# Six projected tiles traced with the first RWKV iterations, another SBUF layout, and GLA and SSD in three passes

## The chip, the cores and the metric

The kernel runs on one core of a Trainium2 chip. The metric is the device time of one execution in microseconds; before the change it is 2274.1 us (median of 3 runs, 2272.3 to 2274.61).

## What is computed

Two layers over 256 context and 1024 image tokens of width 1024. Each layer normalizes, projects once, feeds four token mixers of width 256, and projects back:

```python
hn = rmsnorm(h, p['norm_pre']) * (1.0 + scale) + shift
proj = hn @ p['w_in']
f_rw, f_s5, f_ssd, f_gla = split_last(proj, [...])
y_rw, st_rw = rwkv7_mixer(f_rw, p, grid, ini[0], need_out)
y_s5, st_s5 = s5_mixer(f_s5, p, ini[1], need_out)
y_ssd, st_ssd = ssd_mixer(f_ssd, p, ini[2], need_out)
y_gla, st_gla = gla_mixer(f_gla, p, ini[3], need_out)
y = jnp.concatenate([y_rw, y_s5, y_ssd, y_gla], axis=-1) @ p['w_out']
return h + gate * rmsnorm(y, p['norm_post']), states
```

Every mixer runs forwards and backwards; the context's final states start the image's scan, and layer 1 needs no output for the context. GLA and SSD are chunked linear recurrences (chunks of 64 and 128 tokens): each chunk contributes a state, `S = dec * S + ctb`, and a chunk's output is a term within the chunk plus the query times the state before the chunk. RWKV7 has a recurrence with a rank-one correction, which the kernel solves per window of 128 tokens with a triangular inverse.

## The kernel before

A layer has three stages, `project`, `rw` and `out_proj`, with SBUF pools of their own (`pools`), opened on the left or the right side of SBUF. A pool that opens over a closed one waits, tile by tile, for the old tile's last reader (`reuse_waits="tile"`). All code is traced in program order; the framework's scheduler then fixes one static order of instructions on each engine, which the chip runs in order.

`project` keeps the normalized input split in two fp32r halves (`hi`, `lo`: the tile pool `hn`) and multiplies it with weight tiles that are also split (`i_wh`, `i_wl`): three products, summed in the PSUM bank `pj`. The stage does S5's constants, GLA, SSD and RWKV's shifted projections (order `MO = 'pgsr'`), and at its end the last six tiles: `u0`, `u1` (S5's input), `s5g0`, `s5g1` (its gate), `rwg0`, `rwg1` (RWKV's gate). Results go to DRAM (`f_...`, `rm`). Then `hn` is closed.

GLA before goes through 20 steps `s`. Each transposes keys when needed (`g_kp`), multiplies the query chunk with the state `g_S` (`pc<-g_S,g_e`, one 64x256 program for each direction), adds the result to `g_Y` on VectorE, multiplies keys and values into a contribution (`pc<-l_gv,g_kp`), and forms the next state from PSUM in two products on VectorE (`g_S`, `g_Sd`). SSD does the same in 10 steps, with a state `s_S` that ACT copies out of `s_Sc`.

`rw` runs ten windows in each direction as a software pipeline of 14 iterations: `elem` (decays, `ps<-r_in`, `r_BK`), `pair` (`pb<-r_AD,r_BK`, the matrices `r_A`), the inversion (`r_N`, `r_X`, `r_tp` on VectorE, `pi<-r_DN,r_Am` on TensorE), the chain through the state (`px<-r_UV,r_A`, `px<-r_S,r_AR`, `pu`), and `rw_final`, which norms and gates (`r_yt`, `qfy`) and stores to `yd`. S5's scan runs beside it in pieces.

`out_proj` loads 16 half tiles of `w_out` through a stage of two buffers (`o_w`), splits each (ACT casts `o_w0h`..., POOL or VectorE subtracts to `o_w0l`...), loads `yd` (`o_y`), splits it, and accumulates 192 matmuls for each block of 256 tokens.

Of the kernel before, what the change touches and what calls it, by code (L numbers as in the profile page):

```python
# [15 lines left out]
OP = mybir.AluOpType  # L16
# [219 lines left out]
RL = ('sm rp rl hp tp qp|re rx', 're hp tp qp rx|rp sm rl')  # L236
CL = ('oy oo ob|oa', 'oa oy oo|ob')
# [11 lines left out]

LE = "vvvv"  # L250

AL = "hp sm rp tp qp"


class K:
# [133 lines left out]
    def gla(self, src, outs):  # L389
# [20 lines left out]
        gall, gs = self.S("gall", [128, 2, 20, 4]), self.S("g_gs", [128, 2, 20])  # L410
        k, q = src["gk"], src["gq"]
        for d in range(2):
# [19 lines left out]
            if d == 0:  # L432
                self.tt(g[:, 0:19], l3[:, 0:19], em[:, 1:20], OP.mult)
                nc.vector.tensor_copy(g[:, 19:20], l3[:, 19:20])
            else:
                self.tt(g[:, 0:3], l3[:, 3:0:-1], em[:, 2::-1], OP.mult)
                self.tt(g[:, 3:4], l3[:, 0:1], em[:, 19:20], OP.mult)
                self.tt(g[:, 4:19], l3[:, 19:4:-1], em[:, 18:3:-1], OP.mult)
                nc.vector.tensor_copy(g[:, 19:20], l3[:, 4:5])
            self.tt(gall[:, d], g.unsqueeze(2).to_broadcast([128, 20, 4]),  # L440
                    c("bm4").unsqueeze(1).to_broadcast([128, 20, 4]), OP.mult)
# [7 lines left out]
        Y = [self.T("g_Y", [128, 5, 256]) for _ in range(2)]  # L449
        St = Sp = None  # L450
        for s in range(20):
            ch = [s, 3 - s if s < 4 else 23 - s]
            jb = [x // 2 for x in ch]
            if s % 2 == 0:

                kp = next(kring)
                ps = self.P()
                for d in range(2):
                    nc.tensor.transpose(ps[:, d * 128:(d + 1) * 128], ke[d][:, jb[d] * 128:(jb[d] + 1) * 128], c("ident"))
                p3 = ps[:, :256].rearrange("p (a b) -> p a b", a=2)  # L460
                nc.scalar.copy(kp[0:64, :, 0, :], p3[0:64])
                nc.vector.tensor_copy(kp[64:128, :, 1, :], p3[64:128])
                first = s == 0 if s < 4 else s < 12
                if first and (outs or s >= 4):
                    for j in (jb if jb[0] != jb[1] else jb[:1]):
                        self.gla_pair(j, qe, ke, next(pring), V, Y)
            if s > 0 and (outs or s >= 4):

                ps = self.P("pc")[:, :256]
                for d in range(2):  # L470
                    r = 64 * (ch[d] % 2)
                    self.mm(ps[r:r + 64], qe[d][:, ch[d] * 64:(ch[d] + 1) * 64], St[:, d, :])
                for d in range(2):
                    j, r = jb[d], 64 * (ch[d] % 2)
                    y = Y[j // 5][r:r + 64, j % 5, :]
                    self.tt(y, ps[r:r + 64], y, OP.add)
            if s == 19:
                break
            ps = self.P("pc")[:, :128]
            for d in range(2):  # L480
                j, r = jb[d], ch[d] % 2
                for h in range(4):
                    self.mm(ps[32 * h:32 * h + 32, d * 64:(d + 1) * 64], kp[:, d, r, 32 * h:32 * h + 32], V[j // 5][:, j % 5, h * 64:(h + 1) * 64])

# [28 lines left out]
    def gla_pair(self, j, qe, ke, pa, V, Y):  # L513

        nc, c = self.nc, self.c
        pm = []
        halves = [slice(0, 64), slice(64, 128)]
        for d in range(2):
            qb = self.Q("g_qb", [128, 4, 128])
            self.tt(qb, qe[d][:, j * 128:(j + 1) * 128].unsqueeze(1).to_broadcast([128, 4, 128]),  # L520
                    c("bm4").unsqueeze(2).to_broadcast([128, 4, 128]), OP.mult, "p")
            ps = self.P()[:, :256]
            for h in halves:
                self.mm(ps[h], ke[d][:, j * 128 + h.start:j * 128 + h.stop], qb[:, :, h])
# [7 lines left out]
        ps = self.P()  # L532
        for h in range(4):
            self.mm(ps[:, h * 64:(h + 1) * 64], pa[:, h, :], V[j // 5][:, j % 5, h * 64:(h + 1) * 64])
        nc.scalar.copy(Y[j // 5][:, j % 5, :], ps[:, :256])  # L535


    def ssd(self, src, outs):
# [60 lines left out]
        Y = [self.T("s_Y", [128, 5, 256]) for _ in range(2)]  # L599
        cring = self.ring("s_cp", [128, 2, 128], 2)  # L600
        sring = self.ring("s_S", [128, 2, 256], 2)
# [7 lines left out]
        St = Sp = None  # L609
        for s in range(10):  # L610
            tl = [s, 1 - s if s < 2 else 11 - s]
            if (s == 0 or 2 <= s < 6) and (outs or s >= 2):
                for j in tl:
                    self.ssd_pair(j, B, C, next(cring), xt, stri, lap, dt, Y)
            if s > 0 and (outs or s >= 2):
                ps = self.P("pc")
                for d in range(2):
                    self.mm(ps[:, d * 256:(d + 1) * 256], C[:, tl[d] * 128:(tl[d] + 1) * 128], St[:, d, :])
                yt = self.Q("s_yt", [128, 2, 256])
                for d in range(2):  # L620
                    j = tl[d]
                    y = Y[j // 5][:, j % 5]
                    self.tt(yt[:, d].rearrange("p (h v) -> p h v", h=4), ps[:, d * 256:(d + 1) * 256].rearrange("p (h v) -> p h v", h=4),
                            ex[:, 0, d, j].unsqueeze(2).to_broadcast([128, 4, 64]), OP.mult)
                    self.tt(y, y, yt[:, d], OP.add, "p")
            if s == 9:
                break
            ps = self.P("pc")
            xw = self.Q("s_xw", [128, 2, 4, 64])
            for d in range(2):  # L630
                j = tl[d]
# [6 lines left out]
            p3 = ps[:, :256].rearrange("p (d h v) -> p d h v", d=2, h=2)  # L638
            Sc = self.S("s_Sc", [128, 2, 2, 64], bufs=2)
            if Sp is None:  # L640
                nc.vector.tensor_copy(Sc, p3)
            else:
                self.tt(Sc, Sp, dc[:, :, s].unsqueeze(3).to_broadcast([128, 2, 2, 64]), OP.mult)
                self.tt(Sc, p3, Sc, OP.add)
            Sn = next(sring)
            for g in range(2):
                a = slice(64 * g, 64 * g + 64)
                nc.scalar.copy(Sn[a, :, 128 * g:128 * g + 128].rearrange("p d (h v) -> p d h v", h=2), Sc[a])
            St, Sp = Sn, Sc
# [373 lines left out]
    def rpool(self, name):  # L1023
        return getattr(self, self.where.get(name, "rp"))
# [25 lines left out]
    def rw_proj(self, n, hi, lo, outs):  # L1050
# [6 lines left out]
        for b, (b0, m) in enumerate(BLK):  # L1057
# [4 lines left out]
            o = self.R("i_o", [128, 512], 5)[:, :m]  # L1062
# [32 lines left out]
    def rw_mixed(self, n, kind, o, b0):  # L1095
# [24 lines left out]
    def rw(self, outs, side={}):  # L1120
# [3 lines left out]
        for p, ns in (("re", "in th a cs eP BK AD Ad N X Am tp Rm Bb"), ("rx", "AR A"), ("rl", "ks yt fin f0 yw")):  # L1124
            self.where.update({"r_" + n: p for n in ns.split()})
# [14 lines left out]
        for i in range(10 + 4):  # L1140
            with ExitStack() as es:
# [28 lines left out]
    def rw_elem(self, W):  # L1170
# [62 lines left out]
    def rw_pair(self, W):  # L1233
# [3 lines left out]
        A = self.R("r_A", [128, 2, 4, 2, 128], 3)  # L1237
# [20 lines left out]
        Bt = self.R("r_Bt", [128, 2, 4, 128], 3)  # L1258
# [166 lines left out]
    def rw_final(self, blocks):  # L1425
# [26 lines left out]
        for i, b in enumerate(bs):  # L1452
            nc.sync.dma_start(out=self.yd[self.l][0:256, b * 128:(b + 1) * 128].rearrange("(a p) t -> p a t", p=128), in_=y[:, i])
# [13 lines left out]
    def ada(self, l, part, bank="pz", ring=("a_w", 2)):  # L1467
# [7 lines left out]
        for s in range(8 // nt):  # L1475
# [3 lines left out]
            for k in range(KD):  # L1479
                w = self.R(ring[0], [128, 512], ring[1])  # L1480
# [3 lines left out]
            row = self.R(ring[0], [128, 512], ring[1])[:, :128]  # L1484
# [76 lines left out]
    def proj_ps(self, ws, hi, lo, n):  # L1561
        ps = self.P("pj")[:, :n]
# [8 lines left out]
    def proj(self, names, hi, lo, t0=0):  # L1571
# [30 lines left out]
    def proj_tok(self, name, hi, lo, j0=0):  # L1602
# [6 lines left out]
        for j in range(j0, 10, 2):  # L1609
            o = self.R("i_o", [128, 512], 5)  # L1610
# [102 lines left out]
    def project(self, l, hi, lo, h):  # L1713
# [105 lines left out]
```

## Time and profile before

| what | value |
|---|---|
| median of 3 runs | 2274.1 us |
| profiled execution | 2271.75 us |
| its span | 2269.9 us |
| TensorE, VectorE, ACT, POOL busy | 1970.1, 1571.7, 922.1, 834.8 us |

The stages lie at about 0 to 669 us (`project`, layer 0), 665 to 1080 (`rw`), 1080 to 1217 (`out_proj`), 1217 to 1733, 1736 to 2147 and 2147 to 2270 (layer 1). The busy shares are means over these stages, whose limits differ, so the tables below are by stretch. A matmul's duration reaches into the next one's, since they are pipelined: the time of one is read from the distance between starts.

### The profile page before, as it was taken

The page shows a single profiled execution, that of the slowest core. Times are in us where ns is not written, and L with a number is a line of the kernel's source. Part 1 is how long each engine was busy: PE and PEld are TensorE (multiplying, and loading weights), DVE is VectorE, ACT ScalarE, POOL GpSimd, SP SyncE. Part 2 cuts the span into 40 slices and gives each one's busy share as a digit, 9 for nine tenths or more (in the row PEclk, how much of TensorE's full clock was granted, in tenths as well). Part 3 has the DMA queues.
Part 4 walks back from the last instruction along what each step waited for, and adds up shares of the span by engine and source line. Part 5 has one row for each costly group of instructions (what it writes and reads, how often), then busy time and mean ns, then how long its engine had stood idle before and what let it go on. Part 6 is the DMA issues. An engine that isn't in the chain of part 4 may idle for free. (4 is left out here: it accounts for less than half of the span.)

```text
span 2269.9 us, 44142 instructions
## 1 busy us (share of the span) xinstructions
PE 1970.1 (87%) x17173; PEld 1652.5 (73%) x17176; DVE 1571.7 (69%) x3513; ACT 922.1 (41%) x2005; POOL 834.8 (37%) x947
## 2 busy tenths in 40 slices
PE   7797999999985888888998989999996678787897
PEld 5677788777774777766997777877885567676697
DVE  3876535866638987887477887368563898778654
ACT  3335212244436547544233552123452655564420
POOL 1446431113345535442322266301234355444222
PEclk9899999999997888898999899999998778797998
DMA  8134413454342323214333254234222232220532
GB/s 272 53 117 154 136 58 124 137 180 126 113 130 98 97 68 102 78 36 152 116 108 121 92 175 137 71 105 131 82 75 83 96 94 78 76 71 29 174 110 94
DMA packets 208049, 246.76 MB, mean 109 GB/s; under 512 B 28384, under 2 KB 150240, under 8 KB 207840
## 3 DMA queue, kind: packets, MB, share of 16 engines
q1 hardware_dynamic: 174832, 215.49, 30.4%
q10 hardware_dynamic: 33008, 28.45, 3.8%
q8 instruction: 135, 2.21, 0.4%
q14 instruction: 74, 0.61, 0.1%
HBM read 169.27 MB, written 76.71 MB: 108 GB/s over the span
## 5 line engine op out<-in xcount | busy, mean ns | idle before, releaser
L320 PE MATMUL pj<-hi,i_wh 128*128 128x512 f32 (+1 forms) x952 | 248.4, 381 | 19.2 <-DVE hi L1527 10.8
L320 PE MATMUL pj<-hi,i_wl 128*128 128x512 f32 (+1 forms) x952 | 247.4, 373 | 0.3 <-DVE i_wl L332 0.3
L320 PE MATMUL pj<-lo,i_wh 128*128 128x512 f32 (+1 forms) x952 | 245.9, 375 | 0.0
L320 PEld LDWEIGHTS pj<-hi,i_wh 128*128 128x128 f32 x952 | 169.4, 196 | 54.9 <-DVE hi L1527 11.3
L320 PEld LDWEIGHTS pj<-lo,i_wh 128*128 128x128 f32 x952 | 170.1, 195 | 35.1 <-issue 4.6
L320 PEld LDWEIGHTS pj<-hi,i_wl 128*128 128x128 f32 x952 | 166.6, 192 | 34.4 <-issue 5.0
L332 DVE TENSOR_TENSOR i_wl<-i_w,i_wh 128x512 fp32r<-128x512 f32 x108 | 86.3, 807 | 70.2 <-ACT i_wh L1550 34.4
L1550 ACT CAST i_wh<-i_w 128x512 fp32r<-128x512 f32 x108 | 66.3, 620 | 162.8 <-PE pj L320 127.3
L320 PE MATMUL pb<-r_AD,r_BK 128*128 128x256 f32 x320 | 98.3, 457 | 33.3 <-DVE r_BK L332 14.9
L320 PE MATMUL px<-r_UV,r_A 128*64 128x64 f32 x1216 | 109.4, 248 | 18.8 <-DVE r_UV L1378 9.5
L320 PEld LDWEIGHTS px<-r_UV,r_A 128*64 128x64 f32 x1216 | 93.5, 158 | 41.3 <-DVE r_UV L1378 13.5
L320 PEld LDWEIGHTS pb<-r_AD,r_BK 128*128 128x128 f32 x320 | 70.1, 231 | 47.8 <-POOL r_BK L332 22.8
L1288 DVE TENSOR_TENSOR r_X<-r_X,r_tp 128x30 f32<-128x30 f32 (+1 forms) x300 | 93.2, 311 | 7.7
L332 DVE TENSOR_TENSOR r_tp<-r_N,r_X 128x30 f32<-128x30 f32 (+1 forms) x300 | 91.4, 305 | 7.1
L332 DVE TENSOR_TENSOR g_Y<-pc,g_Y 64x256 f32<-64x256 f32 x70 | 29.4, 421 | 77.1 <-ACT g_Y L535 56.2
L332 POOL TENSOR_TENSOR r_S<-r_S,r_PM 64x256 f32<-64x256 f32 x72 | 54.7, 760 | 72.0 <-DVE r_S L332 66.8
L320 PE MATMUL pj<-i_wh,hi 128*128 128x256 f32 x448 | 71.6, 297 | 9.9 <-ACT i_o L329 5.0
L335 POOL TENSOR_SCALAR r_AD<-r_AR 64x512 f32<-64x512 f32 (+1 forms) x80 | 54.7, 684 | 50.9 <-PE pb L320 34.7
L320 PEld LDWEIGHTS pj<-i_wh,hi 128*128 128x128 f32 x448 | 61.9, 199 | 14.2 <-ACT i_wh L1550 5.6
L329 ACT ACTIVATE r_BK<-r_BK,r_PM 128x128 f32<-128x128 f32 x160 | 58.2, 399 | 31.7 <-PE pb L320 30.6
L332 POOL TENSOR_TENSOR s_Y<-s_Y,s_yt 128x256 f32<-128x256 f32 x34 | 29.1, 868 | 111.0 <-DVE s_Y L332 62.3
L320 PE MATMUL ps<-r_in,rconm 128*128 128x128 f32 x320 | 52.2, 312 | 19.5 <-ACT r_yt L1421 7.7
(466 smaller groups left out, 5156.1 us busy)
## 6 DMA issues: line engine op xcount, KB each, us to landing
i_w<-in_win SPq DMA_DIRECT2D x108, 256.0 KB, 3.0
r_in<-rm SPq DMA_DIRECT2D x36, 512.0 KB, 4.2
a_w<-in_ada SPq DMA_DIRECT2D x64, 256.0 KB, 3.2
rm<-i_o SPq DMA_DIRECT2D x48, 256.0 KB, 2.7
o_y<-yd SPq DMA_DIRECT2D x36, 256.0 KB, 3.2
i_o<-in_ada SPq DMA_DIRECT2D x32, 256.0 KB, 5.2
z_st<-s5t SPq DMA_DIRECT2D x32, 256.0 KB, 2.8
o_w<-in_wout SPq DMA_DIRECT2D x32, 256.0 KB, 2.9
```

Of the source, the lines that this page charges most:

```text
L320: self.nc.tensor.matmul(out, lhsT, rhs, start=start, stop=stop, skip_group_check=True)
L329: self.nc.scalar.activation(out=out, in_=in_, func=f, **kw)
L332: (self.nc.vector if e == "v" else self.nc.gpsimd).tensor_tensor(out, a, b, op)
L335: (self.nc.vector if e == "v" else self.nc.gpsimd).tensor_scalar(out, a, s1, s2, op0, op1)
L1288: last = nc.vector.tensor_tensor(X[:, :, :i, r0:4], X[:, :, :i, r0:4], tmp[:, :, :i, r0:], OP.add)
L1550: self.nc.scalar.copy(hi[:, v], w)
```

## The change

1. The six last tiles leave `project`. They are traced inside `rw`, three after iteration 0 and three after iteration 1 (`LI`), into the PSUM bank `px`. `hn` and the pool `rp` stay open until then; after that `late_pools` opens the pools `rl hp tp qp` in their place.
2. The pools are laid out anew (`RL`, `CL`, `AL`). The tiles that RWKV's rings held (`r_AR`, `r_A`, `r_Bt`, `r_ks`) become tiles named by window, spread over `re` and `rl`. `out_proj`'s weight pool lies over RWKV tiles.
3. GLA and SSD work in three passes: all contributions are copied from PSUM into one array of states (`g_St`, `s_St`); VectorE runs the recurrence in SBUF; then every chunk pair adds its state terms. In GLA these go into the PSUM group of the term within the chunk, as 64x64 matmuls by head (`pc<-g_St,g_qb`), and the output replaces `V`.
4. `i_o` has four buffers instead of five, `a_w` comes from the pool `hp`, and the stores of `r_yt` are issued from POOL's queue instead of SP's.

The counts of program instructions: `pj` matmuls by 768 fewer and `px` by 768 more; `pc<-g_S,g_e` 70 to 0, `pc<-g_St,g_qb` 0 to 280; `pc<-s_S,s_x` 34 to 0, `pc<-s_St,s_cp` 0 to 68.

```diff
-RL = ('sm rp rl hp tp qp|re rx', 're hp tp qp rx|rp sm rl')
-CL = ('oy oo ob|oa', 'oa oy oo|ob')
+RL = ('sm rq re', 'sm re rq')
+RLL = 'rl hp tp qp'
+CL = ('oa oy ob|oo', 'oo ob oy|oa')
+LI = (3, 3)
...
+    def late_pools(self, es, first, side):
+        for s in first:
+            s.close()
+        for n in RLL.split():
+            setattr(self, n, es.enter_context(self.tc.tile_pool(name=n, bufs=1, reuse_waits="tile", side=side)))
...
+            for _ in range(LI[i] if i < len(LI) else 0):
+                next(late)
+            if i == len(LI) - 1:
+                for _ in late:
+                    pass
+                late_pools()
...
-        for s in range(20):
-            ch = [s, 3 - s if s < 4 else 23 - s]
...
-                    self.mm(ps[r:r + 64], qe[d][:, ch[d] * 64:(ch[d] + 1) * 64], St[:, d, :])
...
-                    self.tt(y, ps[r:r + 64], y, OP.add)
...
+            for d in range(2):
+                a = step(d, 2 * j)
...
+                (nc.scalar.copy if d else nc.vector.tensor_copy)(o, ps[:, d])
+        for t in range(19):
+            o = St[t // 10][:, t % 10]
+            if t:
+                self.tt(o, o, St[(t - 1) // 10][:, (t - 1) % 10], OP.add)
+            self.tt(o, o, gs[:, :, t:t + 1].to_broadcast([128, 2, 64]), OP.mult)
...
+                    for h in range(4):
+                        self.mm(ps[64 * r:64 * r + 64, h * 64:(h + 1) * 64], qb[d][:, h, 64 * r:64 * r + 64], St[t // 10][:, t % 10, d], False, d == 1)
...
-                    self.mm(ps[:, d * 256:(d + 1) * 256], C[:, tl[d] * 128:(tl[d] + 1) * 128], St[:, d, :])
+                    self.mm(ps[:, d * 256 + g * 128:d * 256 + g * 128 + 128], cp[:, g], St[(step(d, j) - 1) // 5][:, (step(d, j) - 1) % 5, d].rearrange("p h v -> p (h v)"))
...
-            nc.sync.dma_start(out=self.yd[self.l][0:256, b * 128:(b + 1) * 128].rearrange("(a p) t -> p a t", p=128), in_=y[:, i])
+            nc.gpsimd.dma_start(out=self.yd[self.l][0:256, b * 128:(b + 1) * 128].rearrange("(a p) t -> p a t", p=128), in_=y[:, i])
...
-            for n in ("u0", "u1"):
-                self.proj(n, hi, lo)
-            for n in ("s5g0", "s5g1", "rwg0", "rwg1"):
-                self.proj(n, hi, lo, t0)
+    def late_proj(self, hi, lo, t0):
+        self.where.update({n: "rp" for n in ("i_w", "i_wh", "i_wl", "i_o")})
+        for n in LATE:
+            self.proj(n, hi, lo, 0 if n[0] == "u" else t0, "px")
+            yield
+LATE = ("u0", "u1", "rwg0", "rwg1", "s5g0", "s5g1")
```

TensorE's order of before where RWKV starts in layer 0, from the last projected matmuls to the first inversion (`pi`); `s_Y` is SSD's output.

```order
L320 MATMUL pj<-lo_73,i_wh 128x512 x4
L320 MATMUL pj<-hi_70,i_wl 128x512 x4
L381 MATMUL ps<-con,s_Y 128x128 x5
L320 MATMUL ps<-r_in,rconm 128x128 x4
...
L320 MATMUL pb<-r_AD_6597,r_BK 128x256 x4
L320 MATMUL ps<-r_in,rconm 128x128 x4
L1262 MATMUL pb<-con,r_BK 128x128 x8
L320 MATMUL pb<-r_AD_6597,r_BK 128x256 x4
L320 MATMUL ps<-r_in,rconm 128x128 x8
L320 MATMUL pb<-r_AD_6597,r_BK 128x256 x4
L320 MATMUL pi<-r_DN,r_Am 32x32 x32
```

TensorE's order now at the same place, around the second `pb` group: `hi`, `lo` and `i_w` are the late tiles' operands.

```order
L330 MATMUL px<-hi_69,i_wh 128x512 x4
L330 MATMUL px<-lo_72,i_wh 128x512 x4
L330 MATMUL px<-hi_69,i_wl 128x512 x3
L1263 MATMUL pb<-con,r_BK 128x128 x8
L330 MATMUL px<-hi_69,i_wl 128x512
...
L330 MATMUL px<-lo_71,i_wh 128x256 x4
L330 MATMUL px<-hi_68,i_wl 128x256 x4
L330 MATMUL pi<-r_DN,r_Am 32x32
L330 MATMUL px<-hi_69,i_wh 128x512 x4
...
L330 MATMUL px<-hi_70,i_wl 128x512 x4
L330 MATMUL pi<-r_DN,r_Am 32x32 x31
```

The elementwise and pair matmuls of the first windows, and the first `pi`, now stand among the late tiles, and SSD's output transposes ahead of them.

TensorE's order of before where output projection starts in layer 0; `px<-r_UV,r_A` is the end of the chain, `ps<-...` are the last window's finishing.

```order
L320 MATMUL px<-r_UV_6857,r_A 64x64 x8
L320 MATMUL pj<-o_yh,o_w0h 128x256 x8
L320 MATMUL pj<-o_yh,o_w0l 128x256 x8
L320 MATMUL pj<-o_yl,o_w0h 128x256 x8
L320 MATMUL ps<-con,qfy 64x128 x8
L320 MATMUL pj<-o_yh,o_w1h 128x256 x8
L320 MATMUL pj<-o_yh,o_w1l 128x256 x8
L320 MATMUL pj<-o_yl,o_w1h 128x256 x8
L320 MATMUL pj<-o_yh,o_w2h 128x256 x4
L320 MATMUL ps<-rcon,r_yw 128x128 x4
```

TensorE's order now at the same place, from the chain's end.

```order
L330 MATMUL px<-r_UV_6886,r_A_10287 64x64 x8
L330 MATMUL ps<-con,qfy 64x128 x8
L330 MATMUL ps<-rcon,r_yw 128x128 x4
L330 MATMUL ps<-r_ks_6987,con 128x512
L330 MATMUL ps<-r_yt,con 128x512
L330 MATMUL ps<-con,r_f_10866 128x2 x4
L330 MATMUL ps<-con,qfy 64x128 x8
L330 MATMUL pj<-o_yh,o_w0h 128x256 x8
L330 MATMUL pj<-o_yh,o_w0l 128x256 x8
L330 MATMUL pj<-o_yl,o_w0h 128x256 x8
```

The whole finishing of the last window has moved ahead of the first output matmul.

TensorE's order of before in two GLA steps of layer 0, among the projection matmuls.

```order
L320 MATMUL pj<-hi_69,i_wl 128x512
L320 MATMUL pc<-g_S,g_e 64x256
L320 MATMUL ps<-l_gv,g_pa 128x64 x4
L320 MATMUL ps<-g_qb,g_s 64x256 x4
L320 MATMUL pc<-g_S,g_e 64x256
L320 MATMUL pc<-l_gv,g_kp 32x64 x8
...
L320 MATMUL pj<-hi_70,i_wl 128x512
L320 MATMUL ps<-l_gv,g_pa 128x64 x4
L459 MATMUL ps<-con,g_s 128x128 x2
L320 MATMUL pc<-g_S,g_e 64x256 x2
L459 MATMUL ps<-con,g_s 128x128 x2
```

TensorE's order now, in chunk pairs of GLA in layer 0.

```order
L330 MATMUL ps<-g_qb,g_s 64x256 x2
L330 MATMUL pj<-lo_72,i_wh 128x512 x3
L330 MATMUL pj<-hi_69,i_wl 128x512
L330 MATMUL pc<-l_gv,g_pa 128x64 x4
L330 MATMUL pc<-g_St,g_qb 64x64 x12
L330 MATMUL pc<-l_gv,g_pa 128x64 x4
L330 MATMUL pc<-g_St,g_qb 64x64 x12
...
L330 MATMUL pc<-l_gv,g_pa 128x64 x4
L330 MATMUL pc<-g_St,g_qb 64x64 x16
L330 MATMUL pc<-l_gv,g_pa 128x64 x4
```

The state term, one 64x256 program a direction and step before, is now a run of 64x64 programs behind the term within the chunk, `pc<-l_gv,g_pa`.

## Rows read from the trace of the kernel before

**Rows 1.** Busy time by stretch: stretch, length, each engine busy, clock, DMA

```profile
600.00:650.00 50.00, 50.00 (x347) 38.96 (x346) 16.81 (x39) 18.75 (x37) 14.40 (x21) 1.00 0.33 105
669.50:714.70 45.20, 22.72 (x127) 19.12 (x126) 31.24 (x66) 27.16 (x68) 22.54 (x37) 0.81 0.48 157
714.70:1080.00 365.30, 305.03 (x3730) 253.06 (x3731) 304.38 (x686) 193.93 (x463) 167.43 (x219) 0.85 0.29 88
1080.00:1114.00 34.00, 33.73 (x275) 31.84 (x274) 15.12 (x35) 9.98 (x18) 10.02 (x8) 0.96 0.33 104
1733.50:1792.50 59.00, 26.41 (x132) 22.29 (x132) 39.01 (x85) 27.15 (x66) 27.69 (x39) 0.68 0.35 113
2147.00:2183.00 36.00, 34.73 (x268) 32.06 (x266) 22.13 (x50) 12.16 (x22) 10.83 (x8) 0.91 0.35 110
```

**Rows 2.** TensorE in order of time: start us, duration us, what

```profile
667.50 1.10 PE L320 MATMUL pj<-lo,i_wh 128*128 128x512 f32 x4
668.43 1.09 PE L320 MATMUL pj<-hi,i_wl 128*128 128x512 f32 x4
...
714.68 0.75 PE L320 MATMUL pi<-r_DN,r_Am 32*32 32x32 f32 x64 [0.77 <-DVE r_DN L1293]
...
1732.39 1.10 PE L320 MATMUL pj<-hi,i_wl 128*128 128x512 f32 x4
```

**Rows 3.** Tile `pi` from 1730 us: durations ns, first and last start

```profile
L320 PE MATMUL pi<-r_DN,r_Am x128: 191/191/212, 1792.5 to 1814.6; 32*32 32x32 f32 x128
```

**Rows 4.** TensorE by line, layer 0's gap: busy us, mean ns, idle before

```profile
L320 PE MATMUL pb<-r_AD,r_BK 128*128 128x256 f32 x32 | 11.3, 516 | 16.4 <-DVE r_BK L332 14.9 <-DVE r_A L332 1.4
L320 PE MATMUL ps<-r_in,rconm 128*128 128x128 f32 x56 | 7.8, 284 | 3.3 <-ACT r_a L329 3.3
L381 PE MATMUL ps<-con,s_Y 128*128 128x128 f32 x20 | 2.8, 278 | 1.7 <-DVE s_Y L332 1.7
```

**Rows 5.** The same, layer 1's gap

```profile
L320 PE MATMUL pb<-r_AD,r_BK 128*128 128x256 f32 x32 | 10.1, 463 | 8.9 <-DVE r_tp L332 8.1 <-DVE r_A L332 0.7
L320 PE MATMUL ps<-r_in,rconm 128*128 128x128 f32 x56 | 9.1, 314 | 2.0 <-ACT r_a L329 2.0
L381 PE MATMUL ps<-con,s_Y 128*128 128x128 f32 x16 | 3.9, 426 | 20.0 <-DVE qst L338 18.0 <-DVE s_Y L332 2.0
```

**Rows 6.** TensorE in order of time at four places

```profile
269.29 0.65 PE L320 MATMUL pc<-g_S,g_e 128*64 128x256 f32 x4
269.88 0.43 PE L320 MATMUL pc<-l_gv,g_kp 128*32 128x64 f32 x16
...
641.10 1.03 PE L320 MATMUL pc<-s_S,s_x 128*128 128x256 f32 x4
641.77 1.28 PE L320 MATMUL pj<-lo,i_wh 128*128 128x512 f32 x4
...
735.42 2.08 PE L320 MATMUL px<-r_UV,r_A 128*64 128x64 f32 x32
737.43 0.75 PE L320 MATMUL pi<-r_DN,r_Am 32*32 32x32 f32 x64
...
816.40 1.06 PE L320 MATMUL px<-r_S,r_AR 128*128 128x128 f32 x8
817.29 0.98 PE L320 MATMUL p<-z_us,z_st 128*128 128x160 f32 x6
```

**Rows 7.** Tile `o_w`: durations ns, first and last start

```profile
L1549 SPq DMA_DIRECT2D o_w<-in_wout x16: 327/339/585, 1047.1 to 1094.2; - x16
L1550 ACT CAST o_w5h<-o_w x2: 622/622/622, 1086.3 to 1087.7; 128x512 fp32r<-128x512 f32 x2
L332 DVE TENSOR_TENSOR o_w7l<-o_w,o_w7h x2: 692/692/693, 1096.0 to 1097.6; 128x512 fp32r<-128x512 f32 x2
L1550 ACT CAST o_w7h<-o_w x2: 621/621/621, 1095.4 to 1096.9; 128x512 fp32r<-128x512 f32 x2
```

**Rows 8.** Tile `r_yt`, end of RWKV in layer 0

```profile
L332 POOL TENSOR_TENSOR r_yt<-r_yt,r_fin x2: 1280/1443/1606, 1089.5 to 1114.3; 128x512 f32<-128x512 f32 x2
```

More of the change, by code (lines that the diff above doesn't have):

```diff
@@ new lines, in gla @@
+        St = [self.T("g_St", [128, 10, 2, 64]) for _ in range(2)]
+        step = lambda d, ch: ch if d == 0 else 3 - ch if ch < 4 else 23 - ch
+        for j in range(10):
+            ps = self.P()[:, :256]
+            for d in range(2):
+                nc.tensor.transpose(ps[:, d * 128:(d + 1) * 128], ke[d][:, j * 128:(j + 1) * 128], c("ident"))
+            kp = next(kring)
+            p3 = ps.rearrange("p (a b) -> p a b", a=2)
+            nc.scalar.copy(kp[0:64, :, 0, :], p3[0:64])
+            nc.vector.tensor_copy(kp[64:128, :, 1, :], p3[64:128])
+            ps = self.P("pc")[:, :256].rearrange("p (d r v) -> p d r v", d=2, r=2)
+            for d in range(2):
+                for h in range(4):
+                    for r in range(2):
+                        self.mm(ps[32 * h:32 * h + 32, d, r], kp[:, d, r, 32 * h:32 * h + 32], V[j // 5][:, j % 5, h * 64:(h + 1) * 64])
+            for d in range(2):
+                a = step(d, 2 * j)
+                b = a % 10
+                sl = slice(b, b + 2) if d == 0 else slice(b, b - 2 if b > 1 else None, -1)
+                o = St[a // 10][:, sl, d]
+                (nc.scalar.copy if d else nc.vector.tensor_copy)(o, ps[:, d])
@@ L497, in gla @@
+        for t in range(19):
[3 more added lines that the diff above has]
+            self.tt(o, o, gs[:, :, t:t + 1].to_broadcast([128, 2, 64]), OP.mult)
+        Y = V
+        for j in range(0 if outs else 2, 10):
+            self.gla_pair(j, qe, ke, next(pring), Y, St, step)
         jobs = list(range(0 if outs else 2, 10))
@@ L598, in ssd @@
             nc.vector.tensor_copy(Bt[:, j, :], ps[:, 256:384])
-        Y = [self.T("s_Y", [128, 5, 256]) for _ in range(2)]
+        Y = xt
         cring = self.ring("s_cp", [128, 2, 128], 2)
-        sring = self.ring("s_S", [128, 2, 256], 2)
         dc = self.S("s_dc", [128, 2, 10, 2])
@@ L608, in ssd @@
             nc.scalar.copy(dc[a, 1, 2:10], ex[a, 2, 1, 9:1:-1, h])
[L609 to L617, printed above, removed]
-                    self.mm(ps[:, d * 256:(d + 1) * 256], C[:, tl[d] * 128:(tl[d] + 1) * 128], St[:, d, :])
[L619 to L627, printed above, removed]
+        step = lambda d, j: j if d == 0 else 1 - j if j < 2 else 11 - j
+        St = [self.T("s_St", [128, 5, 2, 2, 64]) for _ in range(2)]
+        for j in range(10):
             ps = self.P("pc")
@@ L1023, in rpool @@
     def rpool(self, name):
-        return getattr(self, self.where.get(name, "rp"))
+        return getattr(self, self.where.get(name, "rq" if name.startswith("r_") else "rp"))
     def rzero(self, name, shape, n):
@@ L1465, in adas, with ada @@
             yield from self.ada(*a)
-    def ada(self, l, part, bank="pz", ring=("a_w", 2)):
+    def ada(self, l, part, bank="pz", ring=None):
         nc, sc = self.nc, self.sc
@@ L1479, in ada @@
             for k in range(KD):
-                w = self.R(ring[0], [128, 512], ring[1])
+                w = self.R(ring[0], [128, 512], ring[1]) if ring else self.H("a_w", [128, 512])
                 nc.sync.dma_start(out=w.rearrange("p (n m) -> p n m", n=nn), in_=src[k, :, :, 128 * nt * s:128 * nt * (s + 1)])
@@ L1483, in ada @@
                     self.mm(ps[32 * q:32 * q + 2, :128], sc[:, k * 2:k * 2 + 2], w[:, 128 * q:128 * q + 128], k == 0, k == KD - 1)
-            row = self.R(ring[0], [128, 512], ring[1])[:, :128]
+            row = (self.R(ring[0], [128, 512], ring[1]) if ring else self.H("a_w", [128, 512]))[:, :128]
             nc.gpsimd.memset(row, 0.0)
@@ L1726, in project @@
                 self.ada_in()
-                for _ in self.ada(0, 0, "pj", ("i_o", 5)):
+                for _ in self.ada(0, 0, "pj", ("i_o", 4)):
                     pass
```

146 lines of the change are left out of this document (60 added, 86 removed).

## The prediction

> **What bounds the kernel now.** I read the table of stretches first. In the second half of the first projection TensorE has no idle time (50.00 of 50, [rows 1]); there every added TensorE microsecond costs one. In RWKV it is busy 305.03 of 365.30 and VectorE 304.38, so neither alone is the limit: the iteration is a chain that passes between them, and an added microsecond on either costs about five sixths or nothing. At the start of output projection TensorE is again full (33.73 of 34.00 in layer 0, 34.73 of 36.00 in layer 1).
>
> The weak places are the two starts of RWKV. The PE timeline gives the ends: the last projected matmuls end at 668.43+1.09 = 669.5 and 1732.39+1.10 = 1733.5, the first inversion matmul `pi<-r_DN,r_Am` starts at 714.68 and 1792.5 [rows 2, 3]. These gaps are 45.2 and 59.0 us long, and TensorE works in them only 22.72 and 26.41 us [rows 1]. What it does there, and for whom it waits, is in the groups by line: mostly `pb<-r_AD,r_BK` behind VectorE's r_BK and r_A [rows 4, 5]. The sum of the change is made from these two gaps, against the profiled execution (2271.75 us; the median of the runs shown is 2274.1, so I add 2.3 at the end).
>
> **1. Late tiles: the gaps are filled.** 768 matmuls (both layers) leave the end of projection and are traced with RWKV's iterations 0 and 1. One 512-column matmul costs 0.233 us (two groups of four start 668.43-667.50 = 0.93 apart, [rows 2]). In layer 0, 280 of them stand between the first `ps<-r_in` of RWKV and the first `pi`: three quarters have 512 columns and a quarter 256, so 210*0.233+70*0.12 (half as many columns, half the time, an estimate) = 57 us. With RWKV's own 12 us that is 69 us of TensorE work. The chain from that first `ps` to `pi` took about 44 us in layer 0 (the gap less its first transposes). So the chain is covered and the `pi` should find its operand ready. In layer 1, 202 matmuls are 42 us, with RWKV's 12 some 54, against a chain of 44 to 56 (there the SSD tail lies in it): I charge a stall of 2 us there and 1 in layer 0; bounds 0 and 15 each, the latter if the chain is as long as the gap of 59.0 minus what was already counted.
>
> What RWKV's start still costs on TensorE before the first `pi`, layer 0: 16 of 28 `ps` programs, 7.8*16/28 = 4.5; 9 of 16 `pb<-r_AD` programs, 11.3*9/16 = 6.4; SSD's 20 output transposes 2.8 and eight of the same kind for r_BK 1.1 [rows 4]. Sum 14.8. The other 9 us (12 `ps`, 7 `pb`, S5) come after the first `pi`; I charge half, 4.6, since RWKV leaves a sixth of TensorE idle and has a start-up of its own (bounds 0 and 9). Gain in layer 0: 45.2-14.8-4.6-1 = 24.8 us. Layer 1: `ps` 9.1*16/28 = 5.2, `pb` 10.1*9/16 = 5.7, transposes 3.9, and all the rest of the stretch, 26.41-10.1-9.1-3.9 = 3.3 [rows 1, 5], together 18.1; 5 behind, 2 of stall: 59.0-18.1-5-2 = 33.9 us. Together **-58.7 us**.
>
> **2. GLA in three passes: more, smaller matmuls where TensorE is full.** A step of before (`pc<-g_S`, four records) takes 269.88-269.29 = 0.59 us [rows 6]; there are 35 such steps in both layers. Each becomes eight 64x64 programs, 16 records. No row is exactly that; `px<-r_UV,r_A` has the same tile and output, 32 records in 737.43-735.42 = 2.01 us, so 1.00 for 16. 35*(1.00-0.59) = **+14.4 us**. Bounds: if four run beside each other as `pc<-l_gv,g_kp` does (16 records, 0.43), 35*(0.43-0.59) = -6; if a small record takes as long as a 64x256 one (0.59/4 = 0.15), 16*0.15 = 2.4 and the sum is +63. I take the nearest row. The VectorE work that goes (70 additions of g_Y, 38 products g_S) buys nothing: TensorE does not wait for it in that stretch.
>
> The trace says that splitting costs 0.41 us a step. The Trainium skill, Perfetto Trace Analysis, section Optimizing Tensor Performance (Matmuls), says that larger matmuls are more efficient than smaller ones where possible; that speaks against this edit, and the rows agree in sign. It gives no price, so by it alone the sum would only be worse than without this term, between 0 and the +63 bound.
>
> **3. SSD.** 17 steps of `pc<-s_S` at 641.77-641.10 = 0.67 become 17 of eight 128x128 records; `px<-r_S,r_AR` has that form, 817.29-816.40 = 0.89 [rows 6]. 17*0.22 = **+3.7 us**. The states' copies (ACT) and recurrences (VectorE) stand beside full TensorE and cost nothing unless their chain ends later than the projection: it has the RW projections in front of it now, and SSD's last output is traced before the late tiles, so I see cover of 85 us. Fewer switches between small and large matmuls may give back some: **-4**, an estimate from some 120 fewer pieces of TensorE's order at about 0.03 us.
>
> **4. SBUF: output projection no longer overlaps RWKV's end.** Before, `o_w` loads run from 1047.1 to 1094.2, beside the last RWKV windows, and the last chain matmul hands over at 1080 to the first `pj<-o_yh`; the last window's finishing (until 1114.3+1.28 on POOL) lies beside these matmuls [rows 7, 8]. Now the weights lie over RWKV tiles that live to its very end. The order has all finishing ahead of the first `pj<-o_yh`, the fp32r casts behind RWKV's last copies on ACT, `o_w0l` behind the last POOL product and store, and the loads behind S5's last store on SP. Price: the last window's finishing runs alone, some ten dependent steps of 1.0 to 1.4 us (its POOL product takes 1.28, [rows 8]), 12 us. Then 16 weight loads through a stage of two: the casts of o_w5h to o_w7h show a pair of halves every (1095.4-1086.3)/2 = 4.6 us [rows 7], so 37 us for eight pairs. The last weight is split 49 us after the chain, the first block ends at 52. Before, finishing and first block were done after 34 (TensorE full, [rows 1]). So +18 us in layer 0, and the same in layer 1, whose TensorE was as full in its first 36 us: **+36 us**. Bounds per layer: 8, if the finishing is covered and the first two loads go early; 28, if each pair takes 6 us. In return VectorE and ACT lose the weight split in RWKV's last windows, eight subtractions of 0.69 a layer [rows 7]; RWKV is five sixths VectorE, half of it counts: **-4**.
>
> **5. Small edits, taken as nothing.** r_yt's stores go from SP's queue to POOL's: behind them on POOL now wait the next window's product and, at the end, `o_w0l`; the issue is short and the finishing is already counted in 4. The i_o ring of four instead of five: its loads come at the very start, where a ring one shorter can cost a few us; a_w's move from a ring of two to six buffers may give as much back. Tiles named per window instead of rings change no instruction.
>
> Sum: -58.7+14.4+3.7-4+36-4 = **-12.6**. I lean a little back to zero, as the bounds of GLA, the finishing and the stalls reach further upwards: -9, so 2262.8 for the profiled execution, **2265 us** by the median.
>
> **The rivals.**
> A, the forecast, a small gain: 0.38, 2252 to 2272.
> B, the filling pays as worked out, output projection loses only 8 a layer and GLA's small matmuls run at 0.43: -58.7+16-6+3.7-8 = -53, or 2221; all of that together is unlikely, midway to the forecast is 2243. For it: the first two stage buffers may be free early. Against: the order puts every cast behind the last copies. 0.20.
> C, slower: the serial output projection takes the place of the gap. It is one mechanism: weights that can neither be loaded nor split until RWKV's tiles are free. At 28 us a layer the loss is 56 and the sum +7; if finishing stretches to 20 us as well, +23: 2281 to 2297. It decides from about 24 us a layer on, where the sum is zero. For it: loads, casts and splits were interleaved with RWKV over 47 us, and all of that moves behind it. 0.27.
> D, TensorE runs in order, so a `pi`, `pb` or `ps` that is not ready holds the late tiles behind it: up to 15 us a layer instead of 1 and 2, so -12.6+27 = +14, 2288. Against: 69 us of work over a 44 us chain. 0.06.
> E, the terms cancel, within 0.2%: 0.09.
>
> **How the numbers follow.** A measurement of this kernel tells 0.2%, 4.5 us, from no change. A lies mostly under 2269.6 but part of it inside the bound: of its 0.38 I give 0.31 to faster, 0.07 to same. B is faster, 0.20. C is slower with 0.26, D with 0.05, E and the edges are same. Faster 0.51, same 0.18, slower 0.31. The range reaches from half of B to the end of C: 2232 to 2298. The likeliest case's own is 2252 to 2272.
>
> **What would show it.** Right: no gap in TensorE between the last `px<-hi` and the first `pi`; the first `pi` about 10 to 20 us earlier in layer 0 although the projections take some 9 us longer; 16 records `pc<-g_St` in about 1.0 us; TensorE idle for some 18 us at each start of output projection, with the casts of o_w as releaser. Wrong: RWKV's windows slower than 34 us apiece (lag not caught up), waits of TensorE inside the late tiles, or weight loads in flight before the last chain matmul.

## The result, and the profile after

The changed kernel takes 2246.4 us (median of 4 runs, 2241.5 to 2254.5) against 2274.4 before: ratio 0.988, 95% interval 0.984 to 0.991. Forecast were 2265, with 2232 to 2298 as the range. The profiled execution's span is 2241.4 us. The sign and the range held. The size did not: the kernel gained three times what was forecast. The experiments show that the sum came out right for a wrong reason, since terms wrong by 10 to 40 us offset each other; that it lies inside the range was luck.

TensorE's order of time in the changed kernel, around the first inversion of each layer (start us, duration us, what). It answers to [rows 2, 3].

```profile
678.96 1.07 PE L330 MATMUL px<-hi,i_wl 128*128 128x512 f32 x4
679.96 0.74 PE L330 MATMUL pi<-r_DN,r_Am 32*32 32x32 f32 x62
680.62 1.56 PE L330 MATMUL pb<-r_AD,r_BK 128*128 128x256 f32 x6
...
1737.21 1.07 PE L330 MATMUL px<-hi,i_wl 128*128 128x512 f32 x4
1738.20 0.75 PE L330 MATMUL pi<-r_DN,r_Am 32*32 32x32 f32 x64
```

The inversion follows the last late matmul without a wait: both gaps are gone. It starts 34.7 us earlier than before in layer 0 (680.0 against 714.7) and 54.3 in layer 1 (1738.2 against 1792.5).

Busy time by stretch after (columns as in [rows 1]): RWKV from the inversion to the chain's end, and the first 57 or 61 us from there, layer 0, then layer 1.

```profile
679.96:1051.20 371.24, 304.57 (x3781) 254.49 (x3782) 306.57 (x686) 198.03 (x472) 168.58 (x227) 0.88 0.28 88
1051.20:1108.00 56.80, 37.98 (x250) 32.60 (x246) 15.39 (x35) 13.45 (x24) 19.16 (x17) 0.85 0.30 93
1738.20:2085.00 346.80, 285.24 (x3665) 236.31 (x3664) 293.62 (x658) 192.54 (x463) 162.28 (x219) 0.91 0.27 82
2085.00:2146.00 61.00, 37.91 (x199) 31.09 (x200) 15.42 (x38) 11.96 (x21) 17.65 (x16) 0.67 0.35 110
```

RWKV itself is as long as before within some 9 us. Output projection, which began with a full TensorE, now begins with 18.8 idle of 56.8 us and 23.1 of 61.0. What it waits for is in the tile view of `o_w` in layer 0 (durations ns, first and last start), to be read beside [rows 7]:

```profile
L1550 SPq DMA_DIRECT2D o_w<-in_wout x16: 327/328/412, 1042.9 to 1101.6; - x16
L1551 ACT CAST o_w0h<-o_w x2: 616/616/617, 1052.0 to 1052.5; 128x512 fp32r<-128x512 f32 x2
L342 POOL TENSOR_TENSOR o_w0l<-o_w,o_w0h x2: 1275/1276/1276, 1071.8 to 1073.0; 128x512 fp32r<-128x512 f32 x2
L1551 ACT CAST o_w1h<-o_w x2: 617/617/617, 1075.8 to 1077.1; 128x512 fp32r<-128x512 f32 x2
L1551 ACT CAST o_w7h<-o_w x2: 617/619/621, 1101.8 to 1104.3; 128x512 fp32r<-128x512 f32 x2
```

The first two half tiles are loaded before the chain's end (1051.2) and cast by 1053, but their subtraction stands behind the last window's finishing on POOL and starts at 1071.8. The other fourteen loads wait for the two stage buffers until then. The last cast is at 1104.3, 53 us after the chain's end. In layer 1 the same subtraction starts at 2112.0, 28 us after the chain's end:

```profile
L342 POOL TENSOR_TENSOR o_w0l<-o_w,o_w0h x2: 1275/1278/1280, 2112.0 to 2113.2; 128x512 fp32r<-128x512 f32 x2
```

TensorE shows the same on its side, here in layer 0:

```profile
1064.84 1.97 PE L330 MATMUL ps<-con,qfy 128*64 128x128 f32 x16 [2.27 <-DVE qfy L348]
1066.74 1.78 PE L330 MATMUL pj<-o_yh,o_w0h 128*128 128x256 f32 x8
1073.12 2.45 PE L330 MATMUL pj<-o_yh,o_w0l 128*128 128x256 f32 x8 [4.60 <-POOL o_w0l L342]
```

So what RWKV's start gains is partly given back. The following table is worked out from the traces: the end of the last projected matmul, the start of the inversion's second group (`pi<-r_DT`), the end of the last `px<-r_UV,r_A` (the chain's end), and the first matmul of the next layer's projection or the span's end. The first column of layer 1 is its projection.

| kernel | gap 0 | RWKV 0 | output 0 | proj. 1 | gap 1 | RWKV 1 | output 1 |
|---|---|---|---|---|---|---|---|
| before | 48.3 | 362.8 | 137.0 | 515.9 | 62.4 | 351.4 | 122.7 |
| changed | 3.5 | 367.9 | 162.5 | 524.4 | 3.9 | 342.2 | 157.1 |

Projection 0 ends at 669.4 before and 679.9 now. The gaps lose 103 us; the two output stages, each measured from the chain's end to its last matmul, take 60 more. The rest is in the projections, 10.5 and 8.5 us longer, and in RWKV.

### The profile page after: what moved, and what is told of

It reads as the page before. It is cut to its first block, busy times and chain, and to the rows that moved or that the text cites. A ratio compares the mean times of both kernels' runs of the same rounds, so it can differ in the third digit from the quotient of the medians.

```text
span 2241.4 us, 45148 instructions
## 1 busy us (share of the span) xinstructions
PE 1947.4 (87%) x17712; PEld 1664.7 (74%) x17712; DVE 1529.2 (68%) x3423; ACT 916.7 (41%) x2009; POOL 846.5 (38%) x965
## 5 line engine op out<-in xcount | busy, mean ns | idle before, releaser
L330 PE MATMUL pj<-hi,i_wh 128*128 128x512 f32 (+1 forms) x696 | 180.2, 379 | 18.3 <-DVE hi L1528 13.2
L330 PE MATMUL pj<-lo,i_wh 128*128 128x512 f32 (+1 forms) x696 | 176.9, 372 | 0.1
L330 PE MATMUL pj<-hi,i_wl 128*128 128x512 f32 (+1 forms) x696 | 174.3, 368 | 2.7 <-DVE i_wl L342 2.7
L330 PEld LDWEIGHTS pj<-hi,i_wh 128*128 128x128 f32 x696 | 124.2, 199 | 43.1 <-DVE hi L1528 13.4
L330 PEld LDWEIGHTS pj<-hi,i_wl 128*128 128x128 f32 x696 | 123.9, 195 | 25.6 <-DVE i_wl L342 3.2
L330 PEld LDWEIGHTS pj<-lo,i_wh 128*128 128x128 f32 x696 | 124.0, 197 | 22.6 <-issue 2.6
L342 DVE TENSOR_TENSOR r_A<-pb,rcon 128x512 f32<-128x512 f32 x80 | 53.5, 682 | 42.2 <-PE pb L330 41.9
L345 POOL TENSOR_SCALAR r_AD<-r_AR 64x512 f32<-64x512 f32 (+1 forms) x80 | 54.4, 680 | 48.9 <-PE pb L330 42.4
L330 PE MATMUL pu<-r_rs,r_TT 128*64 128x128 f32 x320 | 49.2, 303 | 21.1 <-ACT r_rs L1375 20.8
L342 POOL TENSOR_TENSOR o_o<-o_o,o_x 128x512 f32<-128x512 f32 x18 | 23.8, 1323 | 114.7 <-DVE o_o L348 113.5
L330 PE MATMUL pj<-i_wl,hi 128*128 128x256 f32 x448 | 66.8, 289 | 0.2 <-DVE i_wl L342 0.2
```

Source lines behind the costliest of these rows:

```text
L330: self.nc.tensor.matmul(out, lhsT, rhs, start=start, stop=stop, skip_group_check=True)
L342: (self.nc.vector if e == "v" else self.nc.gpsimd).tensor_tensor(out, a, b, op)
L345: (self.nc.vector if e == "v" else self.nc.gpsimd).tensor_scalar(out, a, s1, s2, op0, op1)
```

## The experiments

All medians are of 4 or more runs; the kernel before, run on the same chip each time, took 2270 to 2272 us there.

**Old scans in the changed kernel.** `gla`, `gla_pair` and `ssd` were put back:

```diff
-        for t in range(19):
-            o = St[t // 10][:, t % 10]
...
+        for s in range(20):
+            ch = [s, 3 - s if s < 4 else 23 - s]
```

> The changed kernel with GLA and SSD as before (20 and 10 steps, states in g_S and s_S); late tiles, pools and queues as changed. Theory 1 (the forecast's terms: the small state matmuls cost TensorE 14+4-4 = 14 us, the gap does the rest): 14 us faster than the changed kernel, about 2232. Theory 2 (the three passes save time, since the projection stage no longer takes apart its large matmuls for each scan step): slower, about 2256. The bulk of the first pi in layer 0 stands at 680.0 in the changed kernel: theory 1 says about 671, theory 2 about 688.

2344.6 us, ratio 1.033 (1.030 to 1.035): not 14 us faster but 98 slower than the changed kernel, and slower than before. Late tiles and layout without the new scans lose 75 us. Neither theory had that. The last late matmul ends at 715.9 instead of 679.9, and projection 1 takes 566.7 instead of 524.4: 78 of the 98 us. Another 23 are RWKV of layer 1 (365.6 against 342.2 us), of which more at the split run below. Busy time where SSD's scan ran, first of this kernel, then of the changed one over similar stretches:

```profile
536.00:620.00 84.00, 68.34 (x380) 48.91 (x378) 62.56 (x134) 29.58 (x80) 36.79 (x43) 0.80 0.21 65
1645.00:1735.00 90.00, 77.47 (x384) 60.67 (x383) 62.97 (x132) 34.64 (x91) 39.15 (x45) 0.80 0.15 46
```

```profile
540.00:620.00 80.00, 80.00 (x562) 66.48 (x555) 19.90 (x44) 24.45 (x52) 6.90 (x14) 1.00 0.57 176
1645.00:1735.00 90.00, 89.92 (x453) 76.17 (x452) 39.13 (x81) 39.80 (x78) 28.41 (x38) 1.00 0.41 123
```

With the late tiles moved away, SSD's old scan finds too little beside it: TensorE is idle 15.7 us of 84, and its mean granted clock is 0.80 of the full level there. Before, the six tiles were this cover, as the stores of their results show; SSD's scan ran there from 530.8 to 652.9. Before:

```profile
L317 ACTq DMA_DIRECT2D f_u<-i_o x6: 521/521/597, 547.6 to 592.5; - x6
L317 ACTq DMA_DIRECT2D f_s5g<-i_o x6: 322/326/327, 599.0 to 636.6; - x6
```

With the old scans in the changed kernel, the first of these stores comes after the last state product of SSD:

```profile
L330 PE MATMUL pc<-s_S,s_x x36: 377/483/795, 541.6 to 619.4; 128*128 128x256 f32 x36
L327 ACTq DMA_DIRECT2D f_u<-i_o x6: 520/532/585, 625.8 to 652.4; - x6
```

Before, 377 records of projected matmuls (`pj<-hi`, `pj<-lo`) stand beside SSD's scan; here 68 do. The longest wait of TensorE in this stretch, 6.8 us in all, is for ACT's copies of the state (`s_S`), a step of the serial scan.

**New scans alone.** The same three functions of the changed kernel in the kernel before:

```diff
-        for s in range(20):
-            ch = [s, 3 - s if s < 4 else 23 - s]
...
+        for t in range(19):
+            o = St[t // 10][:, t % 10]
```

> The kernel before with only GLA and SSD in three passes; six tiles at the end of projection, pools and output projection as before. Theory 1: 14 us slower than before, about 2288. Theory 2: about 2264, and the end of the last projected matmul in layer 0 earlier than 669.5 by some 5 us. The gap to the first pi stays 45 us in layer 0 by both.

2244.3 us, ratio 0.988 (0.986 to 0.990): as fast as the whole change. The projected matmuls of layer 0 end at 667.6. The gap of layer 0 stays at 46.4, that of layer 1 falls from 62.4 to 49.0. Theory 2's sign is right and its size too small, and its mechanism is not what the stages show: projection 0 is only 2 us shorter and projection 1 is 5 longer. Of the 21.7 us by which the profiled execution is shorter, 13.4 lie in layer 1's gap. The rest is spread over the other stages, and no run shows its cause.

**Late tiles at the end again.** The changed kernel with

```diff
-LI = (3, 3)
+LI = (0, 0)
...
-            self.proj(n, hi, lo, 0 if n[0] == "u" else t0, "px")
+            self.proj(n, hi, lo, 0 if n[0] == "u" else t0)
...
+            for _ in self.late_proj(hi, lo, t0):
+                pass
...
```

> The changed kernel with the six late tiles traced at the end of projection again, into bank pj; pools, scans and queues as changed. If the filled gaps are the gain (forecast term 1): the gaps of about 45 and 55 us return, TensorE idle about half of each, and the time is 50 to 60 us over the changed kernel, 2300, slower than before, because the loss at output projection stays. If the gain came from the scans: within 15 us of the changed kernel, about 2260.

2291.9 us, ratio 1.010 (1.007 to 1.013), 45 us over the changed kernel. The gaps are back; busy time in them:

```profile
673.30:713.80 40.50, 21.73 (x107) 17.68 (x107) 28.09 (x58) 23.23 (x60) 19.57 (x31) 0.77 0.36 116
1751.60:1791.90 40.30, 22.31 (x103) 18.78 (x102) 24.25 (x56) 22.78 (x58) 11.65 (x21) 0.70 0.26 83
```

Half idle, as in [rows 1]. Against the kernel with only the new scans, this one differs by layout, ring sizes and queues: 47.5 us slower, with output stages of 164.7 and 160.5 against 135.0 and 120.8, together 69.4. RWKV's two stages together are 17 us shorter in it. Three medians make the sum: new scans -25.6, layout +47.5, filling -45.4.

**The split begins on VectorE.**

```diff
-"pv"[m % 2])])
+"vp"[m % 2])])
```

> The changed kernel with VectorE splitting the even weight tiles of output projection and POOL the odd ones (before: the other way round), so the first split, which frees the stage of two, no longer stands behind POOL's last product and store of r_yt. If that queue on POOL held the loads (from 1067.8, when VectorE is through, to 1071.8), the second pair of loads starts 3 to 4 us earlier in each layer and the time falls by 6 to 8 us, to about 2239. If the SBUF layout holds the split until the last window's finishing is over, VectorE's split starts at about 1068.3 and the gain is the same 3 us at most; the loads never start before 1060.

2263.9 us, 17 slower than the changed kernel, where I had expected 6 to 8 faster. The output stages hardly move (164.0 and 154.8). The loss is RWKV of layer 1: 365.3 instead of 342.2 us. Its source is untouched; the scheduler has put its rows into another order (on POOL an `r_AD` scaling has gone ahead of `r_th`, for one). Busy time of this stage, in the changed kernel and then in this one:

```profile
1742.00:2084.30 342.30, 281.42 (x3583) 233.06 (x3582) 292.08 (x655) 189.44 (x456) 161.47 (x217) 0.91 0.27 81
1739.30:2104.60 365.30, 297.37 (x3583) 247.93 (x3582) 294.45 (x656) 189.98 (x454) 161.67 (x217) 0.83 0.24 74
```

As many matmuls are busy for 16 us more, at a mean granted clock of 0.83 instead of 0.91, and 7 us are more idle time. Whether the new order lowers the clock, or the clock differs for another reason, is not shown. Either way a stage that was not edited differs by 23 us, and a total alone can't judge an edit of this size.

The theory itself did not hold. In layer 0 the subtraction moves from 1071.8 to 1065.0, but only from 20.5 to 17.7 us after the chain's end, since VectorE too does its part of the finishing first. It is the finishing ahead of the split, not POOL's queue alone, that holds the weights.

**Weights over tiles that end earlier.**

```diff
-CL = ('oa oy ob|oo', 'oo ob oy|oa')
+CL = ('|oo ob oa oy', '|oo oy ob oa')
```

> The changed kernel with only output projection's pools placed otherwise (layer 0 'oo ob oa oy' and layer 1 'oo oy ob oa', all on the right side), so that the first weights lie over tiles that end earlier and their loads and splits stand ahead of the last window's finishing in the order. Theory: what output projection lost (chain's end to its last matmul 137.0 before, 162.5 changed in layer 0; 122.7 and 157.1 in layer 1) is the wait for SBUF under the weights. Then these two fall to 140 to 150 and 130 to 140 and the time by 30 to 40 us, to about 2210. Rival: the loss is the serial load and split through the stage of two, wherever the weights lie: the stages stay within 5 us of 162 and 157. RWKV's own windows, whose order is decided anew, may move by 10 to 20 us either way; the stages are read apart from them.

2225.4 us, ratio to before 0.980 (0.976 to 0.984), the fastest kernel here, beyond the changed one's interval. The output stages take 157.7 and 134.9, so the theory holds in layer 1 (22 us) and hardly in layer 0 (5), where the subtraction of the fifth tile (`o_w4l`) still stands behind the finishing, until 1068.6, 24 us after the chain's end. Its start of output projection in layer 1:

```profile
2077.88 1.09 PE L330 MATMUL px<-r_UV,r_A 128*64 128x64 f32 x16
2079.20 1.32 PE L330 MATMUL ps<-rcon,r_yw 128*128 128x128 f32 x8 [0.23 <-DVE r_yt L348]
2081.46 1.10 PE L330 MATMUL ps<-r_ks,con 128*128 128x512 f32 x2 [0.94 <-DVE r_yt L342]
2083.34 1.12 PE L330 MATMUL ps<-r_yt,con 128*128 128x512 f32 x2 [0.78 <-DVE r_ks L342]
2087.33 1.66 PE L330 MATMUL ps<-con,r_f 128*128 128x2 f32 x8 [2.87 <-POOL r_f L342]
```

TensorE still has only the finishing to do there, as in the changed kernel, but the weights are split beside it: `o_w4h` is cast at 2080.2, and `o_w7h` follows at 2095.6, 17 us after the chain.

```profile
L1551 ACT CAST o_w4h<-o_w x2: 616/616/617, 2079.7 to 2080.2; 128x512 fp32r<-128x512 f32 x2
L1551 ACT CAST o_w7h<-o_w x2: 618/618/618, 2093.7 to 2095.6; 128x512 fp32r<-128x512 f32 x2
```

**Layer 1 alone, with late weights and with early ones.** Layer 0 has its six tiles at the end and pools like those of before.

```diff
+                if l == 0:
+                    rs.close()
+                    hs.close()
+                    k.pools(ps, *RN, "sm rp rq rl hp tp qp".split(), "re rx".split(), **PS)
+                    k.rw(True, k.s5_jobs(True), iter(()), lambda: None)
```

> New scans in both layers; late tiles inside RWKV and the new layout in layer 1 only; layer 0 has its six tiles at the end of projection and pools like those of before. By stages from the runs so far: layer 0 as in the kernel with only the new scans (to 1210), layer 1 as in the changed kernel (1027 more): 2238. If the two layers are not independent (the order of layer 1 is decided anew), within 15 us of that.

2270.9 us, missed by 33: output 0 and projection 1 together take 687.7 us, where the two runs behind my sum make 659.4 (135.0 with only the new scans and 524.4 in the changed kernel). So the two layers are not independent. In this run TensorE waits 26 us for VectorE's work on S5 (`z_bp`, `z_w`, `z`) before projection 1, which it does not with only the new scans.

> As the run with late tiles in layer 1 only, and layer 1's output pools placed as in the run with early weights ('oo oy ob oa' on the right). Theory of SBUF under the weights: output projection of layer 1 takes 130 to 140 instead of 157, so some 20 us less than that run, about 2218. Rival (serial load and split): no difference.

2256.6 us. Against the run before, only the output pools of layer 1 differ, and output 1 takes 137.7 instead of 157.6, as forecast. The time falls by 14 us and not by 20; its absolute value was missed with the other run's.

**One scan at a time.** Only `ssd` new in the kernel before:

```diff
-            Sn = next(sring)
+        St = [self.T("s_St", [128, 5, 2, 2, 64]) for _ in range(2)]
```

> The kernel before with only SSD in three passes, GLA as before. If the gain of the new scans is the end of SSD's serial scan, which in the kernel before ran until the RWKV start (last scan matmul at 1736.3 in layer 1, gap 62 us): the gap of layer 1 falls from 62 to about 49 us, and the time to about 2255. If it is GLA's part, the gap stays and the time is within 5 us of 2270.

2267.6 us, ratio 0.998 (0.997 to 1.000). The gap of layer 1 fell to 48.2 as expected, the time did not: projections 0 and 1 end up 6 us longer each and RWKV 0 by 5.

Only `ssd` old in the changed kernel:

```diff
-        St = [self.T("s_St", [128, 5, 2, 2, 64]) for _ in range(2)]
+            Sn = next(sring)
```

> The changed kernel with SSD alone as before (10 serial steps through PSUM and ACT), GLA in three passes. With both scans old, the projections took 36 and 42 us longer than in the changed kernel. Theory: what needs the six late tiles beside it is SSD's serial scan; without them TensorE waits for it. Then this run's projections are longer by most of 36 and 42 us, and the time is 2310 to 2345. Rival: GLA's 20 steps were the part that needed cover; then the projections are within 10 us of the changed kernel, and the time below 2270.

2253.3 us, 7 over the changed kernel; projection 0 ends at 673.2 and projection 1 takes 529.7. My theory that SSD by itself is what needs the six tiles fell. Its serial scan runs from 421 to 547 here, ahead of the late tiles too, but with 331 records of other projected tiles beside it:

```profile
421.00:547.00 126.00, 121.16 (x881) 93.88 (x881) 83.05 (x191) 44.05 (x105) 36.68 (x45) 0.97 0.39 118
```

So of the 98 us that both old scans cost the changed kernel, 91 go away with the new GLA alone.

Only `gla` and `gla_pair` new in the kernel before:

```diff
-        St = Sp = None
+        St = [self.T("g_St", [128, 10, 2, 64]) for _ in range(2)]
```

> The kernel before with only GLA in three passes, SSD as before. The run with SSD alone old fell out the other way than I forecast (its projections stayed short), so GLA's serial steps are the part: they last from 254 to 420 us where both scans are old, from 277 to 329 where GLA is new, and SSD comes after them. Theory now: GLA alone carries the gain of the new scans (26 us for both): about 2250, with the gap of layer 1 near 49 us since SSD is through earlier. Rival: neither scan alone does it (SSD alone gave 4 us of the 26): within 6 us of 2271.

2254.1 us, ratio 0.992 (0.990 to 0.994): 16 of the 26 us, with gaps of 46.4 and 48.9. SSD alone gave 4, so GLA is the larger part and some 6 us need both. Its place in time, from the tile view of `pc` in layer 0, first before, then with GLA alone new (durations ns, first and last start):

```profile
L320 PE MATMUL pc<-l_gv,g_kp x304: 219/219/243, 243.0 to 412.7; 128*32 128x64 f32 x152
L320 PE MATMUL pc<-g_S,g_e x76: 379/379/430, 248.8 to 417.8; 128*64 128x256 f32 x76
L320 PE MATMUL pc<-s_xw,s_Bt x72: 272/273/323, 530.8 to 646.0; 128*64 128x128 f32 x72
```

```profile
L320 PE MATMUL pc<-l_gv,g_kp x320: 219/219/243, 241.0 to 263.8; 128*32 128x64 f32 x160
L320 PE MATMUL pc<-g_St,g_qb x304: 222/222/271, 272.1 to 323.9; 128*64 128x64 f32 x152
L320 PE MATMUL pc<-s_xw,s_Bt x72: 272/273/324, 415.2 to 534.9; 128*64 128x128 f32 x72
```

From the first contribution to the last state term GLA took 175 us among the large matmuls (243 to 418); now it takes 83 (241 to 324). SSD comes after GLA and, still serial, ends 111 us earlier. This joins the runs: a long GLA pushes SSD to the end of projection, where few projected tiles but the six are left to stand beside it. In layer 1 of the kernel before it ran until RWKV's start:

```profile
L320 PE MATMUL pc<-s_S,s_x x32: 377/379/483, 1619.3 to 1736.3; 128*128 128x256 f32 x32
```

That is past the last projected matmul (1733.5), which explains the longer gap of layer 1.

## Why the prediction was right in sign and wrong in its terms

**1, the filled gaps: right mechanism, its gain forecast a quarter too large.** Forecast -58.7; the run with the late tiles at the end gives -45.4. The fill leaves no stall (forecast 1 and 2). The work behind the inversion costs more: RWKV 0 is 12.6 and RWKV 1 is 6.2 us longer with the fill, against 4.6 and 5. And 13 of the 14 us by which the gap of layer 1 was longer than that of layer 0 are not the fill's: the new scans remove them by themselves.

**2 and 3, the scans: the step that failed, sign and all.** I forecast +14.1 and measured -25.6. The matmuls are cheaper than the row I chose. The changed kernel's state terms of a chunk pair, 32 records:

```profile
288.41 1.54 PE L330 MATMUL pc<-g_St,g_qb 128*64 128x64 f32 x32
289.88 1.10 PE L330 MATMUL pc<-l_gv,g_pa 128*128 128x64 f32 x8
```

They take 1.47, so 0.74 for 16 instead of 1.00: 35*(0.74-0.59) = +5 and not +14.4. In this run of 32, nine records start only 3 to 6 ns after the one before them and the others 52 ns or more; my row (`px<-r_UV,r_A`) has no such pairs, its records start 58 ns apart. The granted clock was full at both places. The Trainium skill, Perfetto Trace Analysis, section Optimizing Tensor Performance (Matmuls), prefers larger matmuls; on the matmuls alone the trace agrees, by 0.15 us a step. But the price was never in the matmuls. I wrote that a freed VectorE "buys nothing: TensorE does not wait for it in that stretch". TensorE did not wait because other projected tiles stood beside the scans; that said nothing on how long the scans lasted, and SSD's last steps were in layer 1's gap, where I had seen the tail [rows 5] and given its removal to the late tiles. That gap is 13 of the 26 us; where the others come from stays open.

The sentence "cost nothing unless their chain ends later than the projection" held the missing interaction. The six tiles can cover the end of the scans or RWKV's start, not both. With the old scans, late tiles and layout together cost 75 us; with the new ones 2, which is within the noise.

**4, output projection: right place, mis-sized.** Forecast +36, measured +60 by the stages of before and changed (25.5 and 34.4). The finishing, from the chain's end to the subtraction, takes 21 us in layer 0 and 28 in layer 1 and not 12, because each step waits for another engine; the loads take about what was forecast (33 and 37 us from there to the last cast). In layer 1 the first block ends 71 us after the chain. That the weights' place in SBUF is the cause is shown for layer 1 (-22 and -20 us with other pools), and for layer 0 only in part (-5). I had named weight loads ahead of the last chain matmul as a sign of being wrong: in layer 0 two of the sixteen were (1042.9), which gained little, since their split stood behind the finishing. The -4 for the freed VectorE is not separable from the up to 23 us by which RWKV differs between these kernels, nor was the -4 for fewer switches between small and large matmuls measured by itself.

**5, small edits.** Not tried one by one; the layout's 47.5 us contain them.

The terms that I mis-sized offset each other. By the medians the scans were 40 us too dear in my sum, filling 13 and the layout 16 too cheap (47.5 against 36 and -4). So rival C's mechanism happened, at 30 us a layer, above the 24 from which I had let it decide, and did not decide, since the scans paid for it.

## What to carry to other kernels

An engine that is always busy hides how long a serial chain beside it lasts. Before work is moved away from such a chain, look where the chain ends, and measure each of two such edits without the other: here one gave -26 us, the other +75, and both together -28. Under a scheduler that orders all instructions anew, compare stages and their granted clock, and not only totals, since untouched code differed by 23 us.

## What was not expected of the hardware

A store of `r_yt` issued by POOL occupied it for 0.74 us, by SP 0.46 before (median of the issues at the end of layer 0), and landed in 3.7 us instead of 2.1. Now, then before:

```profile
L1454 POOL DMA_DIRECT2D yd<-r_yt x6: 726/738/749, 1035.9 to 1071.0; - x6
DMA to landing us min/median/max: 2.2/3.7/5.2
```

```profile
L1453 SPq DMA_DIRECT2D yd<-r_yt x4: 377/464/503, 1090.8 to 1116.4; - x4
DMA to landing us min/median/max: 2.0/2.1/2.3
```

Why it landed later was not tried. A state record with an output of 64x64 took 46 ns on average in the run of 32 shown above, less than the 58 ns of the row that the forecast used, because nine of them start almost together with the one before.
